# Hyena transforms of a hybrid diffusion block: a length-511 DFT replaced by transforms on half-odd frequencies of folded signals

## The chip, the core and the metric

The program runs on one NeuronCore of one Trainium2 chip. The metric is the device time of one execution in microseconds (us). A program of one core is compared by the median of its runs.

## The reference

The kernel computes two layers of a backbone block for 256 latent tokens and 256 context tokens of width 1024: three token mixers (Hyena long convolution, retention, mLSTM), a gated merge, then a dense feed-forward (layer 0) or eight experts (layer 1). The change concerns the Hyena mixer alone, 384 channels wide, with two orders and a forward and a backward filter for each:

```python
def hyena_filters(length, p):
    ...
    h = hid @ p['hy_f3'].astype(F32)
    window = jnp.exp(-t[:, None] * jnp.abs(p['hy_decay'].astype(F32))[None, :])
    return (h * window).reshape(length, HY_ORDER, 2, HY_W)

def long_conv(u, h_fwd, h_bwd, skip):
    b, l, ch = u.shape
    filt = jnp.concatenate([h_fwd, jnp.zeros((1, ch), F32), h_bwd[1:][::-1]], axis=0)
    u_f = jnp.fft.rfft(u.astype(F32), n=2 * l, axis=1)
    k_f = jnp.fft.rfft(filt, axis=0)
    y = jnp.fft.irfft(u_f * k_f[None], n=2 * l, axis=1)[:, :l]
    return y + u.astype(F32) * skip.astype(F32)

def hyena_branch(u, p):
    ...
    for o, gate in enumerate((x1, x2)):
        z = gate.astype(F32) * long_conv(z, filt[:, o, 0], filt[:, o, 1], p['hy_skip'][o])
    return z
```

## The kernel before

Activations lie transposed: 128 channels on the partitions, tokens along the row. Layer 0 carries 512 tokens (latent and context), layer 1 only the 256 latent ones in its Hyena part. Weights are streamed by DMA, split into a high and a low part by the scalar engine and the vector engine (`two_parts`, L371 and L372), and multiplied in three passes in a reduced fp32 format; the Hyena transforms, the filters and the transposes are plain fp32 matmuls instead. In the trace each plain fp32 matmul appears as two records, a transpose as one.

A build-time scheduler with its own timing model sets the order of the instructions on each engine, from priorities given by the order of the code and a few delays (`later`). On the chip each engine then runs its list strictly in that order. So the Hyena steps, the mLSTM steps (tiles `ml..`) and the projections (`u0rq`, `u0rv` and so on) are interleaved on TensorE, and one can hide the other's waits.

**The filters.** `filter_bank(l, o)` runs once for each layer and order, four times in all. It makes the windowed filters (`fh`, `win`) in two tiles of 128 lags, forms the sum and the difference of forward and backward filter on GpSimd (`fp`, `win`), and transforms them with the DFT matrix `dft`: two kinds (cosine, sine), two tiles of 128 frequencies, two tiles of lags, so 8 matmuls of 384 columns into tiles `pk` (L674). The vector engine scales each result into `K` (L676). Layer 0's two banks run in the first 70 us, among the conditioning products (`mod`, `wm`) and the first projection `u0mv`; layer 1's lie in the dense feed-forward of layer 0.

**The signals.** `hyena()` goes over groups of two blocks of 128 channels by 256 tokens: three groups in layer 0 (block = latent or context of one channel tile), in layer 1 one group of two channel tiles and one of a single tile. For each group and each order `o` it makes one chain, named `hy<layer><group><order>`: transposes (tile `..t`, L1086), a copy to SBUF by the scalar engine (`..zt`, L1088), the forward transform (`..f`, L1095), four products with `K` and a difference and a sum on the vector engine (`..m`, L1108 to L1114), the inverse transform (`..y`, L1120), the skip term and the gate (`..z`, L1127 and L1128, or L1133 and L1135 in layer 1). The next order begins with that result.

Of the kernel before, what the change touches and what calls it, by code (L numbers as in the profile page):

```python
# [11 lines left out]
F32 = mybir.dt.float32  # L12
# [4 lines left out]
ALU = mybir.AluOpType  # L17
# [62 lines left out]
def host_layout(inp):  # L80
# [168 lines left out]
def kernel(ctx: ExitStack, tc: tile.TileContext, A, out):  # L249
# [334 lines left out]
    dft = lcp.tile([P, 2, 512], F32, name="dft", tag="dft")  # L584
# [56 lines left out]
    def filter_bank(l, o):  # L641
# [103 lines left out]
    def layer(l, x, mixed=None, merged=None, done=None, behind=None):  # L745
# [328 lines left out]
        def hyena():  # L1074
            groups = [[(0, c), (1, c)] for c in range(3)] if both else [[(0, 0), (0, 1)], [(0, 2)]]
            for g, blocks in enumerate(groups):
# [3 lines left out]
                for o in range(2):  # L1080
                    nm = f"hy{l}{g}{o}"
                    pt = bank("pb", f"{nm}t")
                    ptv = pt[:, :nb * 256].rearrange("p (t b c) -> p t b c", t=2, b=nb)
                    for b in range(nb):
                        for tt in range(2):
                            PE.transpose(ptv[:, tt, b], z[b][:, tt * P:(tt + 1) * P], ident)  # L1086
# [29 lines left out]
                    for b in range(nb):  # L1116
                        idx = 0
# [854 lines left out]
```

## Time and profile before

| | |
|---|---|
| median of 3 runs | 2101.25 us (2100.95, 2101.25, 2107.12) |
| the profiled execution | 2106.02 us, of which the span from first to last instruction is 2104.2 us |
| TensorE (PE) busy | 2030.8 us, 97% of the span |
| vector engine (DVE) busy | 883.4 us, 42% |
| scalar engine (ACT) busy | 527.5 us, 25% |
| mean granted TensorE clock | 0.98 of full |

Hyena's chains run from 129.6 to about 276 us (layer 0) and from about 1078 to 1155 us (layer 1). In the rows below, a line such as `L1095` is a line of the kernel, `x16` the number of records, and `out<-in` names the tiles by the program's names.

### The profile page before, as it was taken

To read this page: it belongs to the slowest core of one execution; us is meant where nothing else is said; L and a number is where in the kernel's file an instruction comes from. 1 tells how busy PE (TensorE), PEld (TensorE's weight loads), DVE (VectorE), ACT (ScalarE), POOL (GpSimd) and SP (SyncE) were. 2 spreads that over 40 slices of the span, in tenths; PEclk is the share of its full clock that TensorE was granted. 3 is DMA by queue.
4 is the path that set the end of the run, shared out by engine and by line. 5 is a ranking of instruction groups with operands and counts; after the bars stand their busy time and mean duration, and the time that the engine had idled before them with its cause. 6 is when DMAs were issued, how large, how long until landed. Compare 5 with 4: busy or idle time off the path is not lost. (4 is left out here: it accounts for less than half of the span.)

```text
span 2104.2 us, 46609 instructions
## 1 busy us (share of the span) xinstructions
PE 2030.8 (97%) x20349; PEld 1501.1 (71%) x20349; DVE 883.4 (42%) x1841; ACT 527.5 (25%) x897; POOL 129.7 (6%) x178
## 2 busy tenths in 40 slices
PE   7999999999989999999999999899999999999994
PEld 4777787777767788887787899765656565565662
DVE  6766455543564534445775576502021112211023
ACT  4432223223333222323332344301010101101011
POOL 2100000021110000000100013100000000000010
PEclk9999999999999999999899999899999999999996
DMA  8431033444644233334443547799999999999992
GB/s 287 118 93 59 23 99 112 139 124 138 203 121 147 75 100 96 99 96 152 146 146 120 174 143 235 289 354 344 366 346 375 326 403 401 424 424 347 368 409 110
DMA packets 101036, 448.83 MB, mean 213 GB/s; under 512 B 12140, under 2 KB 14254, under 8 KB 73168
## 3 DMA queue, kind: packets, MB, share of 16 engines
q1 hardware_dynamic: 99552, 443.44, 59.7%
q8 instruction: 164, 2.69, 0.5%
q10 hardware_dynamic: 1152, 2.10, 0.3%
q14 instruction: 56, 0.46, 0.1%
q0 software_dynamic: 112, 0.14, 0.1%
HBM read 444.59 MB, written 1.05 MB: 212 GB/s over the span
## 5 line engine op out<-in xcount | busy, mean ns | idle before, releaser
L1662 PE MATMUL yb0e<-m2b0e,hTb0e 128*32 128x256 f32 x3872 | 219.9, 380 | 0.0
L1662 PE MATMUL h0b0e<-m0b0e,gfb0e 128*32 128x256 f32 (+1 forms) x3840 | 209.6, 361 | 0.0
L1662 PE MATMUL h1b0e<-m1b0e,gfb0e 128*32 128x256 f32 (+1 forms) x3984 | 208.2, 361 | 1.1 <-issue 1.1
L1662 PEld LDWEIGHTS h1b0e<-m1b0e,gfb0e 128*32 128x32 f32 x3984 | 130.7, 110 | 71.8 <-issue 6.4
L1662 PEld LDWEIGHTS yb0e<-m2b0e,hTb0e 128*32 128x32 f32 x3872 | 121.8, 110 | 81.5 <-issue 3.4
L1662 PEld LDWEIGHTS h0b0e<-m0b0e,gfb0e 128*32 128x32 f32 x3840 | 124.5, 110 | 71.0 <-issue 10.5
L372 DVE TENSOR_TENSOR fw_l<-fw_f,fw_h 128x768 fp32r<-128x768 f32 (+1 forms) x86 | 85.1, 989 | 134.6 <-ACT fw_h L371 64.2
L1728 DVE TENSOR_TENSOR hsb0e<-hsb0e,h1b0e 128x768 f32<-128x768 f32 (+3 forms) x24 | 19.8, 827 | 266.1 <-PE h1b0e L1662 266.1
L382 PE MATMUL ff<-nfhi,fw_h 128*128 128x512 f32 x328 | 129.6, 395 | 0.6 <-ACT fw_h L371 0.6
L371 ACT ACTIVATE fw_h<-fw_f 128x768 fp32r<-128x768 f32 (+1 forms) x86 | 74.0, 861 | 216.5 <-PE ff L382 110.4
L382 PE MATMUL ff<-nflo,fw_h 128*128 128x512 f32 x328 | 127.5, 389 | 0.0
L372 DVE TENSOR_TENSOR wg_l<-wg_f,wg_h 128x1024 fp32r<-128x1024 f32 (+2 forms) x72 | 86.9, 1209 | 83.2 <-ACT wg_h L371 55.9
L1761 DVE TENSOR_TENSOR ylb0e<-yb0e,yhb0e 32x256 fp32r<-32x256 f32 x88 | 36.9, 420 | 153.4 <-ACT yhb0e L1760 153.0
L371 ACT ACTIVATE wg_h<-wg_f 128x1024 fp32r<-128x1024 f32 (+2 forms) x72 | 69.3, 964 | 116.2 <-DMA wg_f<-in_wg_dram 33.5
L382 PE MATMUL ff<-nfhi,fw_l 128*128 128x512 f32 x328 | 92.1, 389 | 0.0
L382 PE MATMUL ug<-n0hi,wg_h 128*128 128x512 f32 x192 | 76.8, 401 | 0.0
L382 PE MATMUL ug<-n0lo,wg_h 128*128 128x512 f32 x192 | 75.6, 394 | 0.0
L1760 ACT ACTIVATE yhb0e<-yb0e 32x256 fp32r<-32x256 f32 x88 | 33.0, 375 | 160.5 <-PE yb0e L1662 118.0
L382 PEld LDWEIGHTS ff<-nfhi,fw_h 128*128 128x128 f32 x328 | 61.6, 188 | 15.9 <-ACT fw_h L371 1.2
L382 PEld LDWEIGHTS ff<-nflo,fw_h 128*128 128x128 f32 x328 | 61.6, 188 | 13.2
L382 PEld LDWEIGHTS ff<-nfhi,fw_l 128*128 128x128 f32 x328 | 61.6, 188 | 12.9
L1316 POOL TENSOR_TENSOR acc<-acc,gate 128x512 f32<-128x512 f32 (+1 forms) x32 | 46.7, 1478 | 159.0 <-DVE gate L1314 159.0
(1194 smaller groups left out, 3554.0 us busy)
## 6 DMA issues: line engine op xcount, KB each, us to landing
m2b0e<-in_mo_dram SPq DMA_DIRECT2D x88, 1024.0 KB, 8.0
m1b0e<-in_mo_dram SPq DMA_DIRECT2D x59, 1024.0 KB, 7.3
m0b0e<-in_mo_dram SPq DMA_DIRECT2D x56, 1024.0 KB, 9.6
wm_f<-in_wmod_dram SPq DMA_DIRECT2D x70, 512.0 KB, 3.7
wg_f<-in_wg_dram SPq DMA_DIRECT2D x48, 512.0 KB, 4.3
m0b0e<-in_mo_dram SPq DMA_DIRECT2D x32, 768.0 KB, 5.0
m1b0e<-in_mo_dram SPq DMA_DIRECT2D x32, 768.0 KB, 4.7
fw_f<-in_ff_dram SPq DMA_DIRECT2D x56, 384.0 KB, 3.2
```

What stands on the lines that cost most here:

```text
L371: S.activation(hi, src, AF.Copy)
L372: V.tensor_sub(lo, src, hi.bitcast(F32))
L382: PE.matmul(ps, w[:, js], a, start=(n == 0), stop=(n == len(ws.order) - 1))
L1316: G.tensor_add(a_, a_, d)
L1662: PE.matmul(ps[32 * g:32 * g + 32, u * 256:u * 256 + c], stat(u, g), w[:, g * c:(g + 1) * c], start=(first and u % 2 == 0), stop=(last and ...
L1728: V.tensor_tensor(units(t, c, nu), units(t, c, nu), units(ps, c, nu), op=ALU.mult)
L1760: S.activation(yh[rows, at], src, AF.Copy)
L1761: V.tensor_tensor(yl[rows, at], src, yh[rows, at].bitcast(F32), op=ALU.subtract)
```

## The change

The 511-point DFT is replaced by a transform on 256 half-odd frequencies. A signal of 256 tokens is first folded about its middle: `fd` holds the sum of its second half and its reversed first half, and their difference (`back` reads or writes the first half backwards). The cosine part depends on the sums alone, the sine part on the differences alone, so each contracts over 128 values and not over 256. The inverse gives 128 values of an even part and 128 of an odd part, and the two halves of the result are their sum and their difference. The filters are split by even and odd lags: one transform of each is made for 128 frequencies, and the other 128 frequencies follow by adding and subtracting (`kev` is a copy of the even part). The scale moves into the table, so `pcol` loses two columns. The table `dft` grows from 1024 to 1280 values on each partition.

```diff
-    dft = lcp.tile([P, 2, 512], F32, name="dft", tag="dft")
+    dft = lcp.tile([P, 10, P], F32, name="dft", tag="dft")
+    F_AT, I_AT = ((4, 5), (6, 7)), ((4, 8), (6, 9))
+
+    def back(t):
+
+        return t[..., 127::-1]
...
-                PE.matmul(ph[:, :384], h2s[l][:, tt * P:(tt + 1) * P], f[:64], start=True, stop=True)
+                PE.matmul(ph[:, :384], h2s[l].rearrange("p (t two) -> p two t", two=2)[:, tt], f[:64], start=True, stop=True)
...
         for kind in range(2):
-            for i in range(2):
-                pk = bank("pa" if l else "pb", f"pk{l}{o}{kind}{i}")
-                for tt in range(2):
-                    PE.matmul(pk[:, :384], dft[:, tt, kind * 256 + i * P: kind * 256 + i * P + P], pq[tt][kind],
-                              start=(tt == 0), stop=(tt == 1))
-                V.tensor_scalar(kt[:, :, kind * 2 + i, :], pk[:, :384].rearrange("p (c f) -> p c f", c=3),
-                                pcol[:, 6 + i:7 + i], None, op0=ALU.mult)
+            pk = []
+            for odd in range(2):
+                pk.append(bank("pa" if l else "pb", f"pk{l}{o}{kind}{odd}")[:, :384])
+                PE.matmul(pk[odd], dft[:, 2 * odd + kind], pq[odd][kind], start=True, stop=True)
+            ev_ = k5(f"kev{l}{o}{kind}", 384)
+            S.activation(ev_, pk[0], AF.Copy)
+            ev_, od_ = (v.rearrange("p (c f) -> p c f", c=3) for v in (ev_, pk[1]))
+            V.tensor_add(kt[:, :, kind * 2], ev_, od_)
+            if kind == 0:
+                V.tensor_sub(kt[:, :, 1], ev_, od_)
+            else:
+                V.tensor_sub(kt[:, :, 3], od_, ev_)
...
+                    fd = s5(f"{nm}fd")
+                    fdv = fd[:, :nb * 256].rearrange("p (t b c) -> p t b c", t=2, b=nb)
+                    if both:
+                        zz = hyt[0, c0].rearrange("p (b n) -> p b n", b=2)
+                        V.tensor_add(fdv[:, 0], zz[:, :, P:], back(zz))
+                        V.tensor_sub(fdv[:, 1], zz[:, :, P:], back(zz))
+                    else:
+                        for b in range(nb):
+                            V.tensor_add(fdv[:, 0, b], z[b][:, P:], back(z[b]))
+                            V.tensor_sub(fdv[:, 1, b], z[b][:, P:], back(z[b]))
...
-                            for tt in range(2):
-                                PE.matmul(pf[:, i * nb * P:(i + 1) * nb * P],
-                                          dft[:, tt, kind * 256 + i * P:kind * 256 + i * P + P], ztv[:, tt],
-                                          start=(tt == 0), stop=(tt == 1))
+                            PE.matmul(pf[:, i * nb * P:(i + 1) * nb * P], dft[:, F_AT[kind][i]], ztv[:, kind],
+                                      start=True, stop=True)
...
-                                PE.matmul(py[:, b * T:(b + 1) * T], vw(yy)[:, i, b], dft[:, i, kind * 256:kind * 256 + 256],
-                                          start=(idx == 0), stop=(idx == 3))
-                                idx += 1
-                    nz = []
+                                PE.matmul(pyv[:, kind, b], vw(yy)[:, i, b], dft[:, I_AT[kind][i]], start=(i == 0), stop=(i == 1))
+                    zo = s5(f"{nm}z")
                     if both:
-                        zz = hyt[0, c0]
-                        zo = s5(f"{nm}z")
-                        V.scalar_tensor_tensor(zo, zz, C(l, "skip", o * 3 + c0), py, op0=ALU.mult, op1=ALU.add)
-                        V.tensor_mul(zz, zo, hyt[1 + o, c0])
-                        nz = z
+                        zov, sk = zo.rearrange("p (b n) -> p b n", b=2), C(l, "skip", o * 3 + c0)
+                        V.scalar_tensor_tensor(zov[:, :, P:], zz[:, :, P:], sk, pyv[:, 0], op0=ALU.mult, op1=ALU.add)
+                        V.scalar_tensor_tensor(back(zov), back(zz), sk, pyv[:, 0], op0=ALU.mult, op1=ALU.add)
+                        V.tensor_add(zov[:, :, P:], zov[:, :, P:], pyv[:, 1])
+                        V.tensor_sub(back(zov), back(zov), pyv[:, 1])
+                        V.tensor_mul(hyt[0, c0], zo, hyt[1 + o, c0])
```

In layer 1 (`both` false) the fold and the unfolding are issued for each block apart, so on 128 columns each: four folds and eight unfolding steps for a group of two blocks, two and four for the single one.

The scheduler makes a new order from this. Two places matter to what follows. The first is TensorE's list at layer 0's last chain, from its transposes to the first half of its inverse. Before:

```order
L1029 MATMUL ml01n_1467<-mv_640,ml01W_1455 128x65 x2
L1086 MATMUL hy021t<-sq,hy_1545 128x128 x4
L1036 MATMUL ml01i_1475<-ml01Cb,mq_784 128x130 x2
L1095 MATMUL hy021f_2131<-hy021zt,dft 128x256 x4
L1095 MATMUL hy021f_2136<-hy021zt,dft 128x256 x4
L1029 MATMUL ml01n_1486<-mv_640,ml01W_1442 128x65 x2
L1029 MATMUL ml01n_1486<-mv_640,ml01W_1463 128x65 x2
L1029 MATMUL ml01n_1486<-mv_640,ml01W_1442 128x65
L1029 MATMUL ml01n_1486<-mv_640,ml01W_1463 128x65
L1036 MATMUL ml01i_1494<-ml01Cb,mq_784 128x130 x2
L1120 MATMUL hy021y<-dft,hy021m_2141 128x256 x2
```

And now, with the changed kernel's own line numbers:

```order
L1053 MATMUL ml01i_1475<-ml01Cb,mq_784 128x130 x2
L1113 MATMUL hy021t<-sq,hy021fd 128x128 x4
L1046 MATMUL ml01n_1486<-mv_640,ml01W_1442 128x65 x2
L1046 MATMUL ml01n_1486<-mv_640,ml01W_1463 128x65 x2
L1046 MATMUL ml01n_1486<-mv_640,ml01W_1442 128x65
L1046 MATMUL ml01n_1486<-mv_640,ml01W_1463 128x65
L1053 MATMUL ml01i_1494<-ml01Cb,mq_784 128x130 x2
L1121 MATMUL hy021f_2144<-hy021zt,dft 128x256 x2
L1121 MATMUL hy021f_2147<-hy021zt,dft 128x256 x2
L1145 MATMUL hy021y<-dft,hy021m_2150 128x128 x4
```

The six `ml01n` and two `ml01i` matmuls that stood between forward and inverse transform stand ahead of the forward one now, and nothing is left between the two.

The second place is the vector engine's list between the inverse transform of `hy020` and the transposes of `hy021`. Before:

```order
L1020 TENSOR_TENSOR ml01W_1455<-ml01W_1455,ml01s_1446 128x384
L1127 SCALAR_TENSOR_TENSOR hy020z<-hy_1545,cols_81,hy020y 128x512
L1128 TENSOR_TENSOR hy_1545<-hy020z,hy_1548 128x512
L1020 TENSOR_TENSOR ml01W_1463<-ml01W_1463,ml01s_1446 128x384
L1038 TENSOR_TENSOR ml01nb_1474<-ml01i_1475,ff_1115 128x260
```

And now:

```order
L1037 TENSOR_TENSOR ml01W_1455<-ml01W_1455,ml01s_1446 128x384
L1149 SCALAR_TENSOR_TENSOR hy020z<-hy_1545,cols_81,hy020y 128x2x128
L1150 SCALAR_TENSOR_TENSOR hy020z<-hy_1545,cols_81,hy020y 128x2x128
L1151 TENSOR_TENSOR hy020z<-hy020z,hy020y 128x2x128
L1152 TENSOR_TENSOR hy020z<-hy020z,hy020y 128x2x128
L1037 TENSOR_TENSOR ml01W_1463<-ml01W_1463,ml01s_1446 128x384
L1153 TENSOR_TENSOR hy_1545<-hy020z,hy_1548 128x512
L1103 TENSOR_TENSOR hy021fd<-hy_1545 128x256
L1104 TENSOR_TENSOR hy021fd<-hy_1545 128x256
```

Two steps have become seven, and the mLSTM product `ml01W_1463` now stands ahead of the gate.

## Rows read from the trace of the kernel before

**Rows 1.** The page, busy time of an engine over the span, share, instructions.

```profile
PE 2030.8 (97%) x20349; PEld 1501.1 (71%) x20349; DVE 883.4 (42%) x1841; ACT 527.5 (25%) x897; POOL 129.7 (6%) x178
```

**Rows 2.** Busy time by stretch: from:to, length, then as the first line says.

```profile
core 0: us, PE busy (x) PEld busy (x) DVE busy (x) ACT busy (x) POOL busy (x), PEclk, DMA share, GB/s
45.00:50.00 5.00, 4.28 (x75) 3.08 (x68) 5.00 (x18) 2.59 (x5) 1.30 (x1) 1.00 0.88 335
150.00:200.00 50.00, 50.00 (x265) 40.82 (x264) 31.33 (x61) 13.95 (x24) 0.76 (x6) 1.00 0.24 73
200.00:250.00 50.00, 47.97 (x259) 38.91 (x257) 27.55 (x64) 12.45 (x25) 0.00 (x0) 1.00 0.12 34
250.00:255.00 5.00, 5.00 (x16) 3.51 (x16) 1.64 (x3) 0.00 (x1) 0.00 (x0) 0.50 0.01 2
700.00:800.00 100.00, 100.00 (x428) 79.84 (x427) 45.22 (x67) 27.15 (x37) 4.43 (x4) 1.00 0.32 89
1100.00:1150.00 50.00, 49.92 (x353) 40.66 (x351) 29.04 (x72) 10.27 (x21) 1.80 (x10) 1.00 0.37 115
```

**Rows 3.** Single lines: records and duration in ns, minimum, median, maximum.

```profile
L674 PE MATMUL pk<-fp,dft x32: 483/486/590, 34.4 to 730.0; 128*128 128x384 f32 x32
L1095 PE MATMUL hy000f<-hy000zt,dft x16: 377/379/382, 135.2 to 141.9; 128*128 128x256 f32 x16
L1095 PE MATMUL hy110f<-hy110zt,dft x16: 275/275/377, 1133.1 to 1134.9; 128*128 128x128 f32 x16
L1120 PE MATMUL hy000y<-dft,hy000m x16: 377/379/382, 153.0 to 170.0; 128*128 128x256 f32 x16
L1120 PE MATMUL hy110y<-dft,hy110m x8: 379/379/483, 1139.5 to 1141.1; 128*128 128x256 f32 x8
```

**Rows 4.** Timeline of TensorE, unbroken runs: start, duration, engine, line, tiles.

```profile
228.94 3.61 PE L1095 MATMUL hy011f<-hy011zt,dft 128*128 128x256 f32 x16
236.66 2.76 PE L1120 MATMUL hy011y<-dft,hy011m 128*128 128x256 f32 x12
735.81 2.75 PE L674 MATMUL pk<-win,dft 128*128 128x384 f32 x8
1133.11 2.05 PE L1095 MATMUL hy110f<-hy110zt,dft 128*128 128x128 f32 x16
```

**Rows 5.** Timeline of the scalar engine at the first projection's weights.

```profile
48.30 0.88 ACT L371 ACTIVATE w0mv_h<-w0mv_f 128x816 fp32r<-128x816 f32 x1 [1.18 <-DMA w0mv_f<-in_win_dram]
```

**Rows 6.** Timeline of the vector engine, the steps behind an inverse transform.

```profile
258.37 0.75 DVE L1127 SCALAR_TENSOR_TENSOR hy020z<-hy,cols,hy020y 128x512 f32<-128x512 f32 x1 [2.05 <-PE hy020y L1120]
259.15 0.69 DVE L1128 TENSOR_TENSOR hy<-hy020z,hy 128x512 f32<-128x512 f32 x1
259.93 0.56 DVE L1020 TENSOR_TENSOR ml01W<-ml01W,ml01s 128x384 f32<-128x384 f32 x1
1141.55 0.48 DVE L1133 SCALAR_TENSOR_TENSOR hy110z<-hy,cols,hy110y 128x256 f32<-128x256 f32 x1 [0.86 <-PE hy110y L1120]
1142.06 0.42 DVE L1135 TENSOR_TENSOR hy<-hy110z,hy 128x256 f32<-128x256 f32 x1
```

**Rows 7.** Single lines: scans of equal size, L909 forwards and L910 backwards.

```profile
L909 DVE TENSOR_TENSOR_SCAN gr<-zcol,ar x2: 679/679/679, 112.5 to 1059.9; 32x256 f32<-32x256 f32 x2
L910 DVE TENSOR_TENSOR_SCAN gr<-zcol,ar x2: 680/680/680, 113.2 to 1060.6; 32x256 f32<-32x256 f32 x2
```

**Rows 8.** Timeline of TensorE and of the vector engine, chain `hy021` and `hy020`'s inverse.

```profile
251.63 2.07 PE L1120 MATMUL hy020y<-dft,hy020m 128*128 128x256 f32 x4
254.76 3.57 PE L1120 MATMUL hy020y<-dft,hy020m 128*128 128x256 f32 x12
...
266.19 1.45 PE L1029 MATMUL ml01n<-mv,ml01W 128*128 128x65 f32 x12
266.39 0.69 DVE L1109 TENSOR_TENSOR hy021m<-hy021f,K 128x512 f32<-128x512 f32 x1 [1.04 <-PE hy021f L1095]
269.02 1.10 PE L1120 MATMUL hy021y<-dft,hy021m 128*128 128x256 f32 x4 [0.88 <-DVE hy021m L1113]
```

More of the change, by code (lines that the diff above doesn't have):

```diff
@@ L162, in host_layout @@
     t = np.arange(T)
-    ang = 2.0 * np.pi * ((t[:, None] * t[None, :]) % 511) / 511.0
-    dft = np.stack([np.cos(ang), np.sin(ang)], 1).reshape(2, P, 512).transpose(1, 0, 2)
-    out["dft"] = dft
+    k = np.arange(P)
+    dft = []
+    for odd in range(2):
+        ang = np.pi * (((2 * k[None, :] + 1) * (2 * k[:, None] + odd)) % 1024) / 512.0
+        dft += [np.cos(ang) / T, np.sin(ang) / T]
+    ang = np.pi * (((2 * k[None, :] + 1) * (2 * k[:, None] + 1)) % 2048) / 1024.0
+    cm, sm_, sg = np.cos(ang), np.sin(ang), np.where(k % 2, -1.0, 1.0)
+    dft += [cm, sg[:, None] * sm_, sm_, sg[:, None] * cm]
+    dft += [sm_ * sg[None, :], cm * sg[None, :]]
+    out["dft"] = np.concatenate(dft, 1)
     pos = t.astype(f)
@@ L188, in host_layout @@
         c[:, 2 + tt] = tt * P + p
-        c[:, 4 + tt] = -tn[tt * P:(tt + 1) * P]
-        c[:, 6 + tt] = 2.0 / 511.0
-    c[0, 6] = 1.0 / 511.0
+        c[:, 4 + tt] = -tn[tt::2]
     out["pcol"] = c
@@ L670, in filter_bank @@
         for kind in range(2):
-            for i in range(2):
-                pk = bank("pa" if l else "pb", f"pk{l}{o}{kind}{i}")
-                for tt in range(2):
-                    PE.matmul(pk[:, :384], dft[:, tt, kind * 256 + i * P: kind * 256 + i * P + P], pq[tt][kind],
-                              start=(tt == 0), stop=(tt == 1))
-                V.tensor_scalar(kt[:, :, kind * 2 + i, :], pk[:, :384].rearrange("p (c f) -> p c f", c=3),
-                                pcol[:, 6 + i:7 + i], None, op0=ALU.mult)
+            pk = []
+            for odd in range(2):
+                pk.append(bank("pa" if l else "pb", f"pk{l}{o}{kind}{odd}")[:, :384])
[8 more added lines that the diff above has]
+                V.tensor_sub(kt[:, :, 3], od_, ev_)
         Ks[l, o] = kt
@@ L1081, in hyena @@
                     nm = f"hy{l}{g}{o}"
+                    fd = s5(f"{nm}fd")
[8 more added lines that the diff above has]
+                            V.tensor_sub(fdv[:, 1, b], z[b][:, P:], back(z[b]))
                     pt = bank("pb", f"{nm}t")
                     ptv = pt[:, :nb * 256].rearrange("p (t b c) -> p t b c", t=2, b=nb)
-                    for b in range(nb):
-                        for tt in range(2):
-                            PE.transpose(ptv[:, tt, b], z[b][:, tt * P:(tt + 1) * P], ident)
+                    for tt in range(2):
+                        for b in range(nb):
+                            PE.transpose(ptv[:, tt, b], fdv[:, tt, b], ident)
                     zt = s5(f"{nm}zt")
@@ L1115, in hyena @@
                     py = bank("pb", f"{nm}y")
-                    for b in range(nb):
-                        idx = 0
-                        for kind, yy in ((0, yc), (1, ys)):
+                    pyv = py[:, :nb * 256].rearrange("p (k b m) -> p k b m", k=2, b=nb)
+                    for kind, yy in ((0, yc), (1, ys)):
+                        for b in range(nb):
                             for i in range(2):
-                                PE.matmul(py[:, b * T:(b + 1) * T], vw(yy)[:, i, b], dft[:, i, kind * 256:kind * 256 + 256],
-                                          start=(idx == 0), stop=(idx == 3))
-                                idx += 1
@@ L1130, in hyena @@
                     else:
                         for b, (s, c) in enumerate(blocks):
-                            zo = s5(f"{nm}z{b}")
-                            V.scalar_tensor_tensor(zo[:, :T], z[b], C(l, "skip", o * 3 + c), py[:, b * T:(b + 1) * T],
-                                                   op0=ALU.mult, op1=ALU.add)
-                            V.tensor_mul(z[b], zo[:, :T], hyt[1 + o, c][:, :T])
+                            zob, sk = zo[:, b * T:(b + 1) * T], C(l, "skip", o * 3 + c)
@@ L1136, in hyena @@
+                            V.scalar_tensor_tensor(zob[:, P:], z[b][:, P:], sk, pyv[:, 0, b], op0=ALU.mult, op1=ALU.add)
+                            V.scalar_tensor_tensor(back(zob), back(z[b]), sk, pyv[:, 0, b], op0=ALU.mult, op1=ALU.add)
+                            V.tensor_add(zob[:, P:], zob[:, P:], pyv[:, 1, b])
+                            V.tensor_sub(back(zob), back(zob), pyv[:, 1, b])
+                            V.tensor_mul(z[b], zob, hyt[1 + o, c][:, :T])
                 for c in sorted({c for _, c in blocks}):
@@ L1882 @@
         if i == 0:
-            nc.sync.dma_start(dft, A["dft"])
+            nc.sync.dma_start(dft, A["dft"].rearrange("p (a m) -> p a m", m=P))
     whole(more_constants())
```

1 line of the change is left out of this document (removed).

## The prediction

> **What bounds the kernel now.** I read the page's busy times first: TensorE is busy for 97% of the span, the vector engine for 42% [rows 1]. A mean says nothing of one stage, so the next view is the busy time by stretch. In layer 0's Hyena stretch TensorE is busy for 50.00 of 50 us from 150 to 200 us and 47.97 from 200 to 250; in layer 1's for 49.92 of 50; in the feed-forward that holds layer 1's filters for all of 100 [rows 2]. DMA is at 0.12 to 0.37 of its time there, the vector engine at 0.45 to 0.63. There a pass that TensorE does not make is time saved, as long as the order leaves it something else to do. It differs in two places. From 45 to 50 us, among layer 0's filters, TensorE is busy 4.28 of 5 us, the vector engine all of it and DMA 0.88 [rows 2]. And at 250 to 255 us the granted clock is 0.50 [rows 2]: the lower of the two levels, 1.2 GHz, in the middle of the last two chains.
>
> **The price of a pass.** Records overlap, so a duration of 379 ns is no price. In an unbroken run the spacing is (duration of the run less one record) over the records less one. Forward transform, 256 columns: (3.61 - 0.379)/15 = 0.215 us; inverse, 256 columns: (2.76 - 0.379)/11 = 0.216; filter, 384 columns: (2.75 - 0.486)/7 = 0.323; 128 columns: (2.05 - 0.275)/15 = 0.118 [rows 3, 4]. Time follows the columns down to 128, although each record loads its own 128 weights; that holds for the new inverse of 128 columns too.
>
> **What is removed.** *Chains of two blocks* (six in layer 0, two in layer 1; `hy000` stands for all): 16 forward records become 8, worth 8 x 0.215 = 1.72 us; 16 inverse records of 256 columns become 16 of 128, worth 16 x (0.216 - 0.118) = 1.57. Together 3.29, eight times: 26.3 us. *Chains of one block* (two, in layer 1): 16 forward records of 128 columns become 8, 0.94 us; 8 inverse records of 256 become 8 of 128, 0.78. Twice 1.72: 3.4 us. *Filters*: 64 `pk` records (32 on `fp`, as many on `win`) become 32 in four banks, so 8 x 0.323 = 2.6 us in each: 10.3 us. The sum is 40.0 us of TensorE's work. The transposes stay, four in a chain of two blocks.
>
> **What is added.** *Vector engine.* A sum or product of 256 columns takes 0.42 us, a scaled sum 0.48; of 512 columns 0.69 and 0.75 [rows 6]. In layer 0 a chain gets two folds (0.84), and 0.75 + 0.69 behind the inverse becomes 2 x 0.48 + 2 x 0.42 + 0.69 = 2.49: 1.89 more, 11.3 in six. In layer 1 the steps have 128 columns, which no row shows alone; between nothing and 0.42 I take 0.30. Two blocks: four folds 1.2, and 1.8 becomes 8 x 0.30 + 0.84 = 3.24, so 2.64 more; one block half that; four chains 7.9. That is 19.2 us in all, on an engine that is idle for 19 to 22 of each 50 us there [rows 2]. In a chain of two blocks in layer 0 it adds 1.9 us while TensorE's part gets 3.3 shorter, so the chain itself does not grow.
>
> *Reversed operands.* Half of these steps read or write 128 values backwards. The nearest rows are the two scans, forwards 679 ns and backwards 680 [rows 7]; I take no extra cost, with a doubling of the reversed steps (about 10 us of vector time, under the same cover) as the other end. The Trainium skill, page "Vector Engine (DVE) Microarchitecture Reference", section 5.1, lists how the engine streams an operand with a negative step as not measured; the scans bear on it, though a scan may be slower than its stream and so hide a cost.
>
> *Filters elsewhere.* Four scaled copies of a bank become four sums or differences from PSUM, as many instructions on the same columns; the scalar engine gets two copies in each bank, busy for 2.59 of 5 us at 45 and for less in every other stretch of [rows 2]. Nothing on the path. The filters' weights `h2s` are now read at every second element; weights load beside the running pass, so I take nothing, at most the 32 `fh` records by 0.1.
>
> **What is not gained.** *The first bank.* Its passes end before `u0mv`, whose weights' high part was late because its DMA was: the scalar engine waited 1.18 us for `w0mv_f` at 48.30 [rows 5], DMA being at 0.88 [rows 2]. TensorE would only wait longer there: 2.6 us lost. The first queue also carries a quarter more of `dft`, 131 KB at 335 GB/s [rows 2]: 0.4 us. The second bank stands among `u0mv`'s passes, and I count it as gained; the other end is that this also is lost, since the vector engine is full there.
>
> *The last chains of layer 0.* Here the new order leaves less cover. Between the forward and the inverse transform of `hy021` the vector engine's last three products and the difference took from 266.39 to 269.02, 2.6 us; 12 records of `ml01n` and the `ml01i` behind them covered most, and TensorE waited 0.88 [rows 8]. Now they stand ahead of the forward transform, nothing covers, and three tiny mLSTM steps (some 0.2 us each) are queued between the products: a wait of about 3.1 us, 2.2 more. In front of `hy021`'s transposes stand two scaled sums, two sums, `ml01W_1463`, the gate and the fold, 2 x 0.48 + 2 x 0.42 + 0.56 + 0.69 + 0.42 = 3.5 us, against two steps of 1.44; the first waits for `ml01W_1455`, which is queued before it. TensorE has `ml01w`, `ml01n` and `ml01i` meanwhile, some 2.4 us, so I put a wait of 1.0. The inverse of `hy020` waits perhaps 0.3, since its forward transform ends earlier. Together 3.5 us. In layer 1 the new list keeps other passes between each forward and inverse transform (least at `hy111`, as before), so I take no new wait there. If the mLSTM steps turn out to be the later ones anyway, these waits are partly the old ones under a new name, and nothing is lost.
>
> **The sum.** 40.0 - 2.6 - 0.4 - 3.5 = 33.5 us. The profiled execution took 2106.0 us, so 2072.5 for one like it; it lies 4.8 above the median of the runs, 2101.25, and the forecast for the median is **2068**.
>
> **Rivals.** *All of it, and the clock with it.* The slow stretch lies inside the work that shrinks. The 16 inverse records of `hy020` took 2.07 + 3.57 us less one overlap, some 5.5 [rows 8], against 16 x 0.216 = 3.5 at full clock. If the stretch is passed before the clock falls, those 2 us and 1 us of mLSTM passes beside them come on top and the new waits vanish: 40 + 3 = 43, 2058 us. For it: there is less work to be caught by the lower level. Against it: the waits around it get no shorter.
>
> *The vector engine becomes the bound.* In layer 0's stretch it would have some 0.6 x 145 + 11 = 98 us of work in about 125 us. If everything that it gets reaches the path, the sum is 40.0 - 2.6 - 0.4 - 19.2 = 17.8 us: 2083. For it: the waits that there are name the vector and the scalar engine. Against it: it is idle for over a third of every stretch of [rows 2] after 150 us. The end at which the inverse of 128 columns costs as much as one of 256, so that the change does half of what it says, lies near: 40 - 8 x 1.57 - 1.6 - 6.5 = 19 us, 2082; the 128-column row speaks against it.
>
> *Slower: the clock.* Thinner work on TensorE can bring the lower level for longer; at 250 us it came out of 50 us in which TensorE had been idle for only 2 [rows 2]. At half clock each microsecond of TensorE's work costs one more. To end above 2107 it must take some 40 us of work at the lower level beyond the few of before, nearly a third of what is left of layer 0's Hyena stretch; were half of it so, 60 us, the time would be 2128. Against it: the stretch before 200 us has other projections to fill in, and none of its waits. The Trainium skill, "TensorE: Matmul & The Clock Gate", Part 1, has the throttled state as the default, which activity releases; that is the rule by which less work makes the rest slower, and the row at 0.50 agrees with its two levels.
>
> **Chances.** The forecast 0.60, from 2061 to 2076; all of it with the clock 0.17; the vector engine or a dear inverse 0.15; a clock loss that eats the gain 0.04; slower by the clock 0.04. A measurement of this kernel can tell about 0.3%, 6.3 us, from no change. So faster 0.92, the same 0.04, slower 0.04. The range from 2056 to 2084 takes in the first three.
>
> **What would show it.** Right: 32 `pk` records in place of 64; 8 forward records in a chain, and 16 of 128 columns spaced at 0.118 in the inverse; layer 1's retention begins more than 30 us earlier, and everything behind it is shifted alike; a wait of some 3 us at `hy021y`; `u0mv` starts where it did. Wrong: reversed steps clearly over 0.42 us; a clock below 1 over more than 10 us of 130 to 260; new waits in the merge or in the experts, whose weights come by DMA, since I count those stages as moved and not changed.

## The result

| | before | changed |
|---|---|---|
| median in the same comparison | 2104.15 us (4 runs, 2100.95 to 2107.12) | 2071.36 us (4 runs, 2068.96 to 2074.72) |
| the profiled execution; its span | 2106.02 us; 2104.2 us | 2074.72 us; 2072.9 us |

The ratio is 0.985, 95% interval 0.982 to 0.987. The forecast of 2068 lies 3.4 us below the median, and the median lies inside the range. Timed again later (`e8_after_again`) the changed kernel had 2074.59 us, ratio 0.988 (0.986 to 0.990). The gain, forecast as 33.5 us, was thus 32.8 us in the first comparison and 26.8 in the second (against 2101.43 there), and 30.1 by the mean of two traces of each kernel.

The page of the changed kernel, busy times as in [rows 1]: TensorE has 42.6 us less.

```profile
PE 1988.2 (96%) x20237; PEld 1473.0 (71%) x20237; DVE 893.8 (43%) x1901; ACT 530.9 (26%) x905; POOL 134.7 (6%) x178
```

Single lines of the changed kernel, columns as in [rows 3]. The filters have 32 `pk` records, a chain's forward transform 8, and its inverse 16 of 128 columns where there were 16 of 256:

```profile
L686 PE MATMUL pk<-win,dft x16: 483/486/561, 37.9 to 700.6; 128*128 128x384 f32 x16
L1121 PE MATMUL hy000f<-hy000zt,dft x8: 379/379/382, 139.9 to 141.4; 128*128 128x256 f32 x8
L1145 PE MATMUL hy000y<-dft,hy000m x16: 272/275/275, 148.5 to 170.9; 128*128 128x128 f32 x16
```

Its timeline of TensorE, runs and waits of the chains that answer to [rows 4, 8]:

```profile
228.82 1.95 PE L1145 MATMUL hy011y<-dft,hy011m 128*128 128x128 f32 x16
248.80 1.89 PE L1121 MATMUL hy021f<-hy021zt,dft 128*128 128x256 f32 x8
253.43 1.13 PE L1145 MATMUL hy021y<-dft,hy021m 128*128 128x128 f32 x8 [2.74 <-DVE hy021m L1138]
```

By the rule of the prediction the inverse's spacing is (1.95 - 0.275)/15 = 0.112 us and the forward one (1.89 - 0.379)/7 = 0.216, as forecast. In front of `hy021y` TensorE waits 2.74 us (forecast 3.1; before 0.88).

The vector engine's new steps, in layer 0 (timeline; L1149 and L1151 forwards, L1150 and L1152 backwards) and on 128 columns in layer 1 (single lines):

```profile
243.09 0.47 DVE L1149 SCALAR_TENSOR_TENSOR hy020z<-hy,cols,hy020y 128x256 f32<-128x256 f32 x1
243.48 0.47 DVE L1150 SCALAR_TENSOR_TENSOR hy020z<-hy,cols,hy020y 128x256 f32<-128x256 f32 x1
243.87 0.41 DVE L1151 TENSOR_TENSOR hy020z<-hy020z,hy020y 128x256 f32<-128x256 f32 x1
244.20 0.41 DVE L1152 TENSOR_TENSOR hy020z<-hy020z,hy020y 128x256 f32<-128x256 f32 x1
...
245.72 0.42 DVE L1103 TENSOR_TENSOR hy021fd<-hy 128x256 f32<-128x256 f32 x1
```
```profile
L1158 DVE SCALAR_TENSOR_TENSOR hy100z<-hy,cols,hy100y x2: 339/340/340, 1078.4 to 1079.6; 128x128 f32<-128x128 f32 x2
L1160 DVE TENSOR_TENSOR hy100z<-hy100z,hy100y x2: 275/276/278, 1079.2 to 1080.9; 128x128 f32<-128x128 f32 x2
```

Backwards costs what forwards costs. On 128 columns a step takes 0.34 or 0.28 where 0.30 was taken.

The stretches that answer to [rows 2], columns as there. The half clock stands at 255 to 258 us now, and from 45 to 50 us TensorE is busy for 2.13 us where it was for 4.28:

```profile
45.00:50.00 5.00, 2.13 (x42) 0.98 (x30) 4.98 (x18) 1.33 (x2) 1.46 (x2) 0.99 1.00 345
150.00:200.00 50.00, 50.00 (x281) 40.07 (x280) 34.20 (x70) 15.38 (x27) 0.93 (x7) 1.00 0.27 78
200.00:250.00 50.00, 45.97 (x294) 38.29 (x293) 39.26 (x99) 14.21 (x30) 0.00 (x0) 1.00 0.11 33
255.00:258.00 3.00, 3.00 (x11) 3.00 (x11) 2.19 (x5) 1.64 (x3) 0.00 (x0) 0.50 0.00 0
```

**Where the time came from.** Each line runs from one record of TensorE to the next named one (the last `f` counts with its end); the columns are two traces of each kernel (the second ones are `e12_before_again` and `e8_after_again`), the forecast's gain, and the mean of the first two columns less the mean of the next two. All in us.

| stretch | before | again | changed | again | forecast | measured |
|---|---|---|---|---|---|---|
| start to first `u0mq` | 68.50 | 67.53 | 72.45 | 72.93 | +2.2 | -4.7 |
| to first `ret00S` (layer 0's chains, early retention) | 242.16 | 240.28 | 222.52 | 222.34 | +16.2 | +18.8 |
| to first `f` of the dense feed-forward | 376.57 | 378.76 | 376.91 | 376.62 | 0 | +0.9 |
| to last `f` (holds layer 1's filters) | 305.55 | 305.53 | 299.75 | 299.75 | +5.2 | +5.8 |
| to first `u1mv` (norm of layer 1) | 19.08 | 17.92 | 15.44 | 16.01 | 0 | +2.8 |
| to first `ret11rq` (layer 1's chains) | 192.17 | 191.94 | 184.09 | 181.99 | +10.0 | +9.0 |
| to the end of the span | 900.17 | 897.84 | 901.74 | 901.26 | 0 | -2.5 |
| span | 2104.2 | 2099.8 | 2072.9 | 2070.9 | 33.6 | 30.1 |

The forecast's terms by stretch: start 5.2 - 2.6 - 0.4; layer 0's chains 6 x 3.29 - 3.5; layer 1's filters 5.2, its chains 2 x 3.29 + 3.4 (33.6 here for 33.5 by rounding). The chains and layer 1's filters came nearly as forecast, and the first `ret11rq` of layer 1's retention 32 to 33 us earlier. The start did not: it lost 4.7 us where 2.2 were to be gained.

**What stands in the start.** The changed kernel: first the scalar engine, then the vector engine, then TensorE (timeline; in brackets the wait just before).

```profile
49.30 0.88 ACT L378 ACTIVATE w0mv_h<-w0mv_f 128x816 fp32r<-128x816 f32 x1 [3.26 <-DMA w0mv_f<-in_win_dram]
50.20 0.26 ACT L490 ACTIVATE modrow<-mod 128x128 f32<-128x128 f32 x1
```
```profile
58.50 0.17 DVE L459 TENSOR_TENSOR lg_r<-lg_r,lg_q 128x12 f32<-128x12 f32 x1
58.59 0.16 DVE L492 TENSOR_TENSOR modT<-mod,cols 128x8 f32<-128x8 f32 x1
59.00 1.38 DVE L749 TENSOR_SCALAR n0h<-n0h,amix,modT 128x256 f32<-128x256 f32 x4
```
```profile
44.05 2.25 PE L488 MATMUL mod<-wm,sT 128*32 128x128 f32 x64
...
50.24 1.27 PE L817 MATMUL u0mv<-w0mv_h,n0hi 128*128 128x272 f32 x4 [2.88 <-ACT w0mv_h L378]
...
53.84 0.27 PE L491 MATMUL mod<-sq,modrow 128*128 128x128 f32 x1
...
58.80 0.64 PE L512 MATMUL mod<-wm_f,sT 128*32 128x256 f32 x8 [2.16 <-DVE modT L492]
```

TensorE has the fourth modulation piece ready at 46.3 us, but its copy `modrow` is queued behind `w0mv_h`, which waits 3.26 us for its DMA; its transpose comes at 53.84, 7.5 us later, and `modT`, which needs only that, another 4.7 later, behind a chain of tiny `lg_r` steps. The second half of `n0h`, which `u0mv` needs, waits for it. In the kernel before, the same two steps, on the scalar and on the vector engine, stood ahead of `w0mv_h` [rows 5] and of the `lg_r` chain:

```profile
46.84 0.28 ACT L483 ACTIVATE modrow<-mod 128x128 f32<-128x128 f32 x1 [1.03 <-PE mod L481]
51.02 0.15 DVE L485 TENSOR_TENSOR modT<-mod,cols 128x8 f32<-128x8 f32 x1
```

In the changed kernel TensorE runs at the lower of its two levels, 1.2 GHz, for part of two stretches, and it is busy for only 2.84 us between them (last columns: granted clock, DMA share, GB/s):

```profile
50.00:55.00 5.00, 4.76 (x27) 4.76 (x28) 4.93 (x9) 1.23 (x4) 3.03 (x3) 0.67 0.34 111
55.00:60.00 5.00, 2.84 (x26) 2.21 (x26) 4.62 (x20) 1.02 (x3) 1.71 (x2) 1.00 0.37 110
60.00:65.00 5.00, 4.39 (x16) 2.94 (x15) 4.85 (x17) 5.00 (x14) 0.00 (x0) 0.66 0.57 149
```

### The profile page after: what moved, and what is told of

It is laid out like the page before. It is cut to its first block, busy times and chain, and to the rows that moved or that the text cites. A ratio compares the mean times of both kernels' runs of the same rounds, so it can differ in the third digit from the quotient of the medians.

```text
span 2072.9 us, 46466 instructions
## 1 busy us (share of the span) xinstructions
PE 1988.2 (96%) x20237; PEld 1473.0 (71%) x20237; DVE 893.8 (43%) x1901; ACT 530.9 (26%) x905; POOL 134.7 (6%) x178
## 5 line engine op out<-in xcount | busy, mean ns | idle before, releaser
L512 PE MATMUL mod<-wm_f,sT 128*32 128x256 f32 x560 | 49.0, 393 | 9.4 <-DMA wm_f<-in_wmod_dram 7.2
```

Source lines behind the costliest of these rows:

```text
L512: PE.matmul(pm[32 * g:32 * g + 32, 0:256], sT[:, k], w[g // 2][:, g % 2 * 256:g % 2 * 256 + 256], start=(k == 0), stop=(k == KD - 1))
```

## The experiments

Every edit makes the scheduler write a new list, so each run is read by stretch. Medians are in us; a ratio is to the kernel before on the same chip, with its 95% interval; the other columns are stretches of the table above.

| run | median (runs) | ratio | to `u0mq` | to `ret00S` | to last `f` | norm | layer 1's chains |
|---|---|---|---|---|---|---|---|
| `e1_big_load` | 2102.60 (10) | 1.0007 (0.9996 to 1.0017) | 71.59 | 240.71 | 303.94 | 16.38 | 192.08 |
| `e2_signals_alone` | 2079.78 (4) | 0.9897 (0.9882 to 0.9912) | 69.62 | 225.24 | 304.67 | 15.21 | 185.73 |
| `e3_filters_alone` | 2093.27 (8) | 0.9964 (0.9954 to 0.9975) | 67.59 | 242.39 | 299.75 | 14.94 | 194.49 |
| `e4_load_split` | 2067.08 (5) | 0.9831 (0.9815 to 0.9848) | 67.61 | 222.56 | 299.75 | 15.04 | 184.60 |
| `e5_inverse_twice` | 2100.60 (10) | 0.9995 (0.9985 to 1.0005) | 72.84 | 243.06 | 301.34 | 15.08 | 192.43 |
| `e6_folds_twice` | 2091.26 (4) | 0.9939 (0.9919 to 0.9958) | 71.46 | 229.15 | 299.75 | 15.22 | 196.78 |
| `e7_load_late` | 2070.04 (5) | 0.9844 (0.9822 to 0.9866) | 65.69 | 225.21 | 299.75 | 15.30 | 182.82 |
| `e8_after_again` | 2074.59 (4) | 0.9879 (0.9863 to 0.9895) | 72.93 | 222.34 | 299.75 | 16.01 | 181.99 |
| `e9_rk_before_rv` | 2076.15 (6) | 0.9892 (0.9872 to 0.9912) | 65.52 | 234.07 | 300.66 | 16.72 | 188.17 |
| `e10_folds_twice_early` | 2075.70 (4) | 0.9885 (0.9865 to 0.9905) | 73.23 | 227.12 | 299.75 | 14.90 | 182.21 |
| `e11_folds_twice_late` | 2069.11 (4) | 0.9849 (0.9828 to 0.9870) | 71.07 | 224.00 | 299.74 | 14.80 | 180.14 |
| `e12_before_again` | 2102.15 (10) | 1.0005 (0.9990 to 1.0021) | 67.53 | 240.28 | 305.53 | 17.92 | 191.94 |

**The longer load alone.**

```diff
-    out["dft"] = dft
+    out["dft"] = np.concatenate([dft.reshape(P, 1024), dft.reshape(P, 1024)[:, :256]], 1)
...
-    dft = lcp.tile([P, 2, 512], F32, name="dft", tag="dft")
+    dft = lcp.tile([P, 1280], F32, name="dft", tag="dft")
+    dft_all, dft = dft, dft[:, :1024].rearrange("p (a m) -> p a m", a=2)
...
-            nc.sync.dma_start(dft, A["dft"])
+            nc.sync.dma_start(dft_all, A["dft"])
```

> The kernel before, with one edit: the table's load has 1280 values on each partition as in the changed kernel, of which it uses its own 1024. Theory A (order at the start): the longer load alone moves the scalar engine's copy modrow of the fourth modulation piece behind w0mv_h, which waits for its DMA, and the vector engine's modT behind the start of the lg chain; so the first u0mq record comes 2 to 5 us later than in the kernel before (68.5 us there), and the whole is 2 to 5 us slower. Theory B (the new filter work itself is what cost the start): first u0mq within 0.5 us of 68.5, the whole the same. Theory C (the bytes alone): 0.4 us later.

The first `u0mq` came at 71.59, 3.1 and 4.1 us later than in the two traces of before: 131 KB more in one load put another list in place, and `modrow` does stand behind `w0mv_h` in it. So much of theory A holds. The path that it names does not: `modrow` waited for TensorE and not for `w0mv_h`. TensorE's timeline shows two waits for filter steps `K` of the vector engine, and then the modulation piece at half clock (64 records in 3.64 us, 1.96 in the kernel before); the last line is the scalar engine's:

```profile
44.28 0.91 PE L659 MATMUL fh<-f,h 64*128 64x384 f32 x2 [1.52 <-DVE K L677]
46.40 1.64 PE L659 MATMUL fh<-f,h 64*128 64x384 f32 x2 [1.21 <-DVE K L677]
47.98 3.64 PE L481 MATMUL mod<-wm,sT 128*32 128x128 f32 x64
51.68 0.28 ACT L483 ACTIVATE modrow<-mod 128x128 f32<-128x128 f32 x1 [0.43 <-PE mod L481]
```

So even `u0mv` began late here, at 53.69 (49.24 and 48.28 in the two traces of before). Nor was the whole 2 to 5 us slower, as theory A had it, but the same: from the first `u0mq` on this execution took 2029.5 us, the two of before 2035.7 and 2032.3, though nothing was edited there.

**Signals alone, filters alone.**

```diff
 # e2: the changed kernel with
+            for i in range(2):
+                pk = bank("pa" if l else "pb", f"pk{l}{o}{kind}{i}")
+                for tt in range(2):
+                    PE.matmul(pk[:, :384], dft[:, 2 * tt + kind], pq[tt][kind], start=(tt == 0), stop=(tt == 1))
+                V.tensor_scalar(kt[:, :, kind * 2 + i, :], pk[:, :384].rearrange("p (c f) -> p c f", c=3),
+                                pcol[:, 6 + i:7 + i], None, op0=ALU.mult)
...
 # e3: the kernel before with the changed filter_bank, its tables taken as
+                PE.matmul(pk[odd], dft[:, 0, (2 * odd + kind) * P:(2 * odd + kind) * P + P], pq[odd][kind], start=True, stop=True)
```

> The changed chains with the filter bank of before (8 matmuls of 384 columns in a bank and four scaled copies; its tables are blocks of the new table, so the values of K are others than the reference's). Theory A: the start is lost as with the longer load alone (first u0mq at 71 to 74 us); from there layer 0's chains give 19 to 20 us, layer 1's 8 to 10, the filters nothing: some 2075 to 2082 us. Theory B: first u0mq at 68.5, the whole 2070 to 2075. If the chains give less than 24 us in all, their 29.7 us were mis-sized, not the start.

> The chains of before with the changed filter bank (4 matmuls in a bank, kev copies, sums and differences; it takes its tables from the columns of the old one, so the values of K are others than the reference's; the load is the old one of 1024). Layer 1's two banks give 5.2 us, in the feed-forward, under every theory. Theory A: modrow stands behind w0mv_h in this order too, so the first u0mq is not earlier than in the kernel before, rather 0 to 4 us later: the whole 2096 to 2103 us. Theory B: the start is lost by the bank's own work, first u0mq at 71 to 73. The forecast as written (one bank of layer 0 gained): first u0mq at 66, the whole 2094.

The gains, 2101.40 - 2079.78 = 21.6 and 2101.40 - 2093.27 = 8.1, add to 29.7 us, which lies between the 32.8 and the 26.8 that the two together gave. The start of `e2` fits theory A only by half (69.62). Its chains gave 16.0 us in layer 0 and 6.3 in layer 1, 22.3 in all and below the 24 that the expectation set; yet from the first `hy000t` to the first `hy021y` TensorE's order is that of the changed kernel, whose two traces gave 18.8 and 9.0. What differs is the granted clock, 0.75, 0.84 and 0.72 in the three stretches of 5 us from 235 to 250, where the changed kernel has 1.00. In layer 1 TensorE's order is the same too. So the shortfall is not the size of the passes: one order of TensorE's records can take some 3 us more or less. In `e3` layer 1's filters give the whole 5.8 us, but the start ends at 67.59, against 68.50 and 67.53 before: of the 5.2 us of passes that layer 0's two banks lose, half a microsecond or so arrives. `modrow` stands behind `w0mv_h` here too, and the start was not lost by it; so that order alone is not the cause, nor is the bank's own work (theory B). The whole, 2093.27, is the 2094 of the forecast as written, but by the norm stretch and not by the start. TensorE, having fewer passes, waits for others:

```profile
58.07 0.77 PE L805 MATMUL u0mv<-w0mv_h,n0hi 128*128 128x272 f32 x4 [1.18 <-ACT n0hi L371]
67.59 0.47 PE L397 MATMUL u0mq<-n0hi,w0mq_h 128*128 128x512 f32 x1 [1.44 <-DVE gc L858]
```

**The load split, and late.**

```diff
         if i == 0:
-            nc.sync.dma_start(dft, A["dft"].rearrange("p (a m) -> p a m", m=P))
+            nc.sync.dma_start(dft[:, 0:4], A["dft"][:, 0:4 * P].rearrange("p (a m) -> p a m", m=P))
     whole(more_constants())
+    nc.sync.dma_start(dft[:, 4:10], A["dft"][:, 4 * P:].rearrange("p (a m) -> p a m", m=P))   # e4; in e7 behind proj("mk")
```

> The changed kernel with the table's load in two: the filters' 4 blocks where the load stands, the signals' 6 blocks behind all the modulation pieces. In this order modrow stands ahead of w0mv_h again and modT ahead of the lg chain. Theory A: first u0mq 4 to 6 us earlier than in the changed kernel (72.45), at 66.5 to 68.5, everything behind shifted alike, the whole 2065 to 2068 us. Theory B: at most 1.3 us (the 393 KB that no longer pass ahead of w0mv_f), the whole 2070 or more.

> As the split load, with the signals' 6 blocks loaded behind the weights of u0mv, u0mq and u0mk instead of ahead of them. If DMA is what holds u0mv (393 KB at some 330 GB/s pass ahead of w0mv_f in the split load): u0mv begins 1.2 us earlier than there, at 48.8, and so does all behind it; some 2066 us. If it is held by the modulation pieces or the normalised x: no change against the split load, 2067.

> The changed kernel itself once more, for a second trace and for times beside the split loads on one chip: 2071 us, within 3. If the start's loss belongs to the order, first u0mq is again at 71.5 to 73, and the low clock at 50 to 65 us is there again; if it belonged to that one execution, first u0mq is near 68.5.

That the order loses the start holds here, and theory B's 1.3 us at most does not. With a short load in front the list has `modrow` ahead of `w0mv_h` again and `modT` ahead of the `lg` chain, and the first `u0mq` comes at 67.61 and 65.69, 4.8 to 7.2 us earlier than in the two traces of the changed kernel, both of which lose the start alike (72.45, 72.93). `e4` on the scalar engine, the vector engine and TensorE, and its first stretch of 5 us behind 50 us:

```profile
46.16 0.26 ACT L490 ACTIVATE modrow<-mod 128x128 f32<-128x128 f32 x1
49.03 0.88 ACT L378 ACTIVATE w0mv_h<-w0mv_f 128x816 fp32r<-128x816 f32 x1 [2.61 <-DMA w0mv_f<-in_win_dram]
```
```profile
49.25 0.15 DVE L492 TENSOR_TENSOR modT<-mod,cols 128x8 f32<-128x8 f32 x1
```
```profile
49.97 1.27 PE L817 MATMUL u0mv<-w0mv_h,n0hi 128*128 128x272 f32 x4 [2.32 <-ACT w0mv_h L378]
```
```profile
50.00:55.00 5.00, 5.00 (x22) 5.00 (x23) 5.00 (x8) 3.39 (x7) 4.65 (x4) 0.50 0.27 86
```

The last row speaks against one rival, the clock: the lower level stands in this start too, and yet the start came back. Over the traces the last `modT` of the start and the first `u0mq` go together: 51.02 and 68.50, 50.06 and 67.53 in the kernel before, 49.25 and 67.61 in `e4`, 48.24 and 65.69 in `e7`, 54.26 and 69.62 in `e2`, 56.25 and 71.59 in `e1`, 58.59 and 72.45, 57.55 and 72.93 in the changed kernel. Only `e3`, with fewer passes behind it, has a late one (54.21) and a start of 67.59. `modT` was not moved by itself, so its share of the loss is argued and not shown.

In `e7` `u0mv` begins at 48.45 without waiting (expected 48.8): DMA held it. But of that gain 2.7 us went again between 230 and 245 us, at a mean clock of 0.86, 0.80 and 0.66, although TensorE's records up to the first `hy021y` have the changed kernel's order; there the clock stayed up until 255. The whole, 2070.04, missed the 2066 expected, and `e8` came 3.6 us above its 2071, with the lower level in its start again (0.66 from 50 to 55 us). The version to keep is a split load: 2067.08 us in its own comparison, and `e7` against `e8` on one chip 0.9844 against 0.9879, intervals that just touch. On the whole time the gain of the split is thus barely clear of the noise; in the start it is clear. Which of the two splits is the faster is not settled.

**Doubling what was removed and what was added.**

```diff
 # e5                for b in range(nb):
-                            for i in range(2):
+                            for i in (0, 1, 0, 1):
                                 PE.matmul(pyv[:, kind, b], vw(yy)[:, i, b], dft[:, I_AT[kind][i]], start=(i == 0), stop=(i == 1))
 # e6; e10: 2 only if both and (g, o) < (1, 1); e11: only if both and (g, o) >= (1, 1)
+                    for _ in range(2):
+                        if both:
+                            V.tensor_add(fdv[:, 0], zz[:, :, P:], back(zz))
+                            V.tensor_sub(fdv[:, 1], zz[:, :, P:], back(zz))
...
```

> The changed kernel with every inverse matmul issued twice (the second pair starts the sum anew, so the values stay): 96 more matmuls, 192 records of 128 columns in layer 0's six chains... counted in records as in the forecast: 16 more in each chain of two blocks, 8 more in each of one, 144 in all, at 0.112 to 0.118 us 16 to 17 us of TensorE. Theory A (TensorE sets the pace in both Hyena stretches): 2085 to 2089 us, 10 to 11 us more from the first u0mq to layer 0's retention and 5 to 6 in layer 1. Theory B (the vector engine or the chains' own length sets the pace, so that passes hide in waits): under 5 us more, below 2077. Theory C (fuller TensorE keeps its clock): 2 to 4 us of A come back, 2081 to 2084.

> The changed kernel with every fold issued twice: 8.4 us more on the vector engine (6 x 0.84 in layer 0, 12 x 0.28 in layer 1), nothing more on TensorE. Theory A (the vector engine's work lies beside TensorE's): less than 1.5 us more, the one pair ahead of hy021's transposes at most 0.84 of it; 2071 to 2073. Theory B (it has become the bound): the 8.4 us reach the time, 2079.

Every theory that I had put down for these two fell. The 144 records added in `e5` are 16 to 17 us of passes; the time grew by 26 to 29, 20.6 of it up to `ret00S` (243.06 against 222.4) for 11.0 of passes. The 8.4 us of vector work in `e6` cost 17 to 20: 6.7 in layer 0 for 5.0, and 13.7 in layer 1 for 3.4. TensorE in `e5`, at layer 0's last two chains:

```profile
256.11 3.81 PE L1145 MATMUL hy020y<-dft,hy020m 128*128 128x128 f32 x32 [1.22 <-DVE hy020m L1138]
264.05 1.08 PE L1113 MATMUL hy021t<-sq,hy021fd 128*128 128x128 f32 x4 [4.13 <-DVE hy021fd L1103]
265.82 3.78 PE L1121 MATMUL hy021f<-hy021zt,dft 128*128 128x256 f32 x8 [0.69 <-ACT hy021zt L1115]
```

As I read it, the longer inverse makes the chain longer and leaves TensorE nothing to put beside it: it stands idle for 4.13 us, and `hy021f` behind that takes 3.78 us where it took 1.89, at half clock. In `e6` TensorE waited 4.66 us for `hy111m` in layer 1. How much of the surplus in either run is the new list and how much the clock was not tested apart. To see whether it is the last chains that are bare, I doubled the folds of the first three and of the last three apart, and gave TensorE other work for the last ones:

```diff
 # e9, with the load of e7
-        proj_tok("rv", rv_evac)
         proj("rk", rk_evac, 512)
+        proj_tok("rv", rv_evac)
```

> The changed kernel with the folds issued twice in layer 0's first three chains alone (hy000, hy001, hy010), 2.5 us of vector work. Theory D (there TensorE is never without other passes): layer 0's retention begins within 0.7 us of 268.5, the whole 2071 to 2075. Theory B (vector work counts anywhere): 2.5 us later.

> The same in layer 0's last three chains alone (hy011, hy020, hy021), again 2.5 us of vector work. Theory D: all of it and more, since each wait is followed by the lower clock: layer 0's retention begins 2.5 to 6.5 us later than 268.5, the whole 2074 to 2080. As the forecast had it (only the pair ahead of hy021's transposes shows): at most 0.84 us later.

> The late load, and in both layers the projection u0rk issued ahead of u0rv, so that TensorE has passes which need none of the chains' PSUM banks while the last chains run (before, the last quarter of u0rv used the chains' own pair of banks and could not start). Theory D (the last chains of layer 0 are exposed: TensorE has nothing else, and the clock falls behind the waits): the 6.8 us of idle and 1.6 us of lower clock between 205 and 265 us in the changed kernel shrink by 3 to 6 us; 2063 to 2067 us, against 2067 to 2070 for the two split loads. Theory E (the passes are only moved, what waits in the last chains waits anyway): 2068 to 2071.

Theory D fell as well, and it fell the other way round. In the last chains 2.5 us of vector work cost 1.6 (224.00 against 222.43), in the first three 4.7 (227.12). But not in place: in `e10` the first `hy010f` still lies 0.1 us from where its start would put it. The loss comes behind that, in chains without any edit, where the new list has put mLSTM's `ml01kds` among the steps that unfold `hy010`, and no longer ahead of them. By the mark that the expectations set, layer 0's retention (first `ret00rq`) at 268.5, `e10` stands at 273.88 and `e11` at 268.46: the start of `e11` was 1.4 to 1.9 us shorter, and its whole, 2069.11, is no longer than the changed kernel's. `e10`, and under it the same place in the changed kernel:

```profile
213.98 2.02 PE L1147 MATMUL hy010y<-dft,hy010m 128*128 128x128 f32 x16 [1.46 <-DVE hy010m L1140]
...
218.30 1.16 PE L1007 MATMUL ml01C<-mv,ml01kds 128*128 128x130 f32 x8 [1.64 <-DVE ml01kds L1001]
...
240.20 3.20 PE L1123 MATMUL hy020f<-hy020zt,dft 128*128 128x256 f32 x8
```
```profile
213.04 0.66 PE L987 MATMUL ml0ot<-sq,ml0hs 128*128 128x128 f32 x4 [1.51 <-DVE ml0hs L860]
...
213.75 2.01 PE L1145 MATMUL hy010y<-dft,hy010m 128*128 128x128 f32 x16
215.60 1.06 PE L1007 MATMUL ml01C<-mv,ml01kds 128*128 128x130 f32 x8
```

Two waits of 1.46 and 1.64 stand for one of 1.51, and further on `hy020f` runs at the lower clock (3.20 for 1.9); that is some 3 of the 4.7 us. `e9` gave layer 0 nothing: from the first `u0mq` to the first `f`, 234.07 + 366.06 = 600.1 us, in the changed kernel 222.52 + 376.91 = 599.4 (in `e7`, from which it was made and which had lost 2.7 us to the clock, 604.7). `u0rv` now waited 3.7 us for the copy of `rk`, and layer 1 lost 4 to 6 us. The passes were only moved, as theory E has it; the time, 2076.15, is above what either theory gave.

**The kernel before, once more.**

> The kernel before once more, for a second trace. If the long norm stage of layer 1 in its first trace (12.05 us from the first n1ss to the first u1mv, 9.58 in the changed kernel) is that execution's clock and not the program, it is some 9 to 10 us here; if it is the program's, 12 again. The stretch at half clock near 250 us should come again if it belongs to the waits there.

From the first `n1ss` to the first `u1mv` it took 11.74 us, near the 12 that stand for the program. So those 2.8 us are not one execution's clock. They are not the change's passes either: `e3`, with the chains of before, has 14.94, and `e1`, with its filters too, 16.38. Half of them is one wait, of `u1mv` for the scalar engine's `n1hi`: 1.5 us in both traces of before, 1.6 in `e9`, 0.6 or less in all others. Why it goes stays open. The half clock came again, behind 256 us and not at 250, and for half as long as in the first trace, with the same program:

```profile
256.00:258.00 2.00, 2.00 (x17) 2.00 (x18) 0.41 (x1) 0.00 (x0) 0.00 (x0) 0.87 0.00 0
258.00:260.00 2.00, 2.00 (x8) 1.70 (x8) 0.91 (x3) 0.60 (x1) 0.00 (x0) 0.50 0.00 0
260.00:262.00 2.00, 2.00 (x9) 1.69 (x8) 1.01 (x5) 0.00 (x0) 0.00 (x0) 0.77 0.00 0
```

## Why the prediction was right, and where it was not

*The price of a pass* held: 0.216 and 0.112 us by the spacing. Layer 0's chains gave 18.8 of their 19.7 us, layer 1's 9.0 of 10.0, layer 1's filters 5.8 for 5.2.

*The last chains of layer 0*: the loss of 3.5 us was too large. The wait before `hy021y` is there (2.74), those before `hy021t` and `hy020y` are not (the list of waits has neither). The stretch at half clock ran from 250 to 256 us in the first trace of before and is down to 255 to 258. But that much is the luck of the first trace: in the second it lasted no longer than in the changed kernel, and with the second traces layer 0's chains gave 17.9 and not 19.6. So the rival "all of it, and the clock with it" is not shown.

*What is not gained* is the step that failed, though the total came out. I counted the first bank as hidden and the second as gained, net 2.2 us. Neither bank gave more than half a microsecond (`e3`), since the stretch waits for the vector engine, the scalar engine and DMA. And the longer load, put at 0.4 us by its bytes, cost the start 3 to 4 by the list that it brought about (`e1`, by another path); with the rest of the change the start lost 4.7, which the split load gives back (`e4`, `e7`). `u0mv` started some 1 us later than it had (50.24 and 49.19, before 49.24 and 48.28); it was its second half that came late. I looked at the start's first record and not at the place of `modT` in the vector engine's list.

*Layer 1's chains*: the forecast saw no new wait. There are some, for DMA: TensorE reaches modulation weights before they land, which from the first `u1mv` to the first `ret11rq` makes 2.8 and 3.6 us of waiting in the two traces of the changed kernel and none in the two of before. The changed kernel, and then `e8`, the same program:

```profile
1097.99 0.64 PE L512 MATMUL mod<-wm_f,sT 128*32 128x256 f32 x8 [0.83 <-DMA wm_f<-in_wmod_dram]
1099.85 0.64 PE L512 MATMUL mod<-wm_f,sT 128*32 128x256 f32 x8 [1.22 <-DMA wm_f<-in_wmod_dram]
...
1101.73 3.42 PE L1145 MATMUL hy101y<-dft,hy101m 128*128 128x128 f32 x16
```
```profile
1099.92 0.64 PE L512 MATMUL mod<-wm_f,sT 128*32 128x256 f32 x8 [0.62 <-DMA wm_f<-in_wmod_dram]
...
1101.57 2.05 PE L1145 MATMUL hy101y<-dft,hy101m 128*128 128x128 f32 x16
```

The waits are much the same, the clock fell in one execution and not in the other.

*Everything behind shifted alike*: nearly. The rest of the program is 2.5 us longer in the changed kernel (mean of two traces each). DMA is at 0.98 to 1.01 of its time where the experts begin, in both kernels; why the rest is longer was not tested.

*Slower by the clock*: no. Up to layer 0's last chain the lower level stands only in parts of 50 to 55 and 60 to 65 us and from 255 to 258. It did not take the gain; what it took of the start is open, since `e4` met it there and lost nothing.

*The vector engine off the path*: true for the change as made, and not as a rule. Its folds and unfolding took what the forecast had (1.86 us more in a chain of layer 0 for 1.89), while its busy time grew by only 10.4 us, not 19.2, mostly since neighbouring records overlap: back to back these steps start 0.33 to 0.39 us apart and last 0.41 to 0.47.

The total was nearer than its terms, and that is luck: the norm stretch (2.8), which is not the change's, and layer 0 (2.6) made up for most of what the start missed (6.9).

## What to carry to other kernels

Price a pass by the spacing of its records, and count it as time only where the stretch's windows show TensorE without a gap; where another engine or DMA is full, count nothing, and look for what is queued behind the longest wait in the new list. Such a price held here for taking work away from a full TensorE; putting passes back cost more than they measure (26 to 29 us for 16 to 17), with another list and a lower clock behind its waits. Load a table in the order of its use: a load that grew by 131 KB moved the whole start, and splitting it gave 4.8 us or more of the start back. And take a second trace before a clock is read into a difference.

## What the runs showed of the hardware

- An operand that is read or written backwards cost nothing on the vector engine in these steps (fp32, 256 columns): 0.47 and 0.47, 0.41 and 0.41 us forwards and backwards; a scaled sum is followed 0.39 us later, a sum 0.33. The Trainium skill, "Vector Engine (DVE) Microarchitecture Reference", section 5.2, gives 1.0417 ns a column and some 75 ns an instruction, by which 256 columns would follow at an estimated 0.34; the sums agree, the scaled sums take some 0.05 more.
- The granted clock is part of the luck of an execution. One order of TensorE's records in layer 1 (`e2`, `e4`, `e7`, `e8`, `e10` and the first trace of the changed kernel) took 182.0 to 185.7 us, and in the kernel before the fall came at 250 us once and behind 256 the other time.
- Waits on TensorE were followed by the lower level of the clock: 2.88 us before `u0mv`, then a mean of 0.67 from 50 to 55 us; 2.74 before `hy021y`, then 0.50 from 255 to 258; 4.13 before `hy021t` in `e5`, then `hy021f` at twice its time. It also fell with less: at 250 us in the first trace of before, behind waits of at most 0.82. The Trainium skill, "TensorE: Matmul & The Clock Gate", Part 1, has the throttled state as the default, which activity releases; these rows agree, and the same list with and without the fall shows that the program alone does not settle it.
